# The normalised inputs of a hybrid encoder layer: rebuilt for every projection, or kept in DRAM as two fp16 parts

## The chip, the cores and the metric

One core of a Trainium2 chip. The metric is the device time of one execution in microseconds (us). The engines are TensorE (PE, with its weight loads PEld), VectorE (DVE), ScalarE (ACT), GpSimd (POOL) and SyncE (SP, which here only issues DMAs); 16 DMA engines move data between SBUF and DRAM.

## The reference

One layer of an encoder trunk and a final RMSNorm, on two requests: "p" with 2048 tokens and "s" with 4096, model width 1024, all in fp32.

```python
h = rms_norm(x, norm_g)
proj = h @ w_in                      # columns are split among three groups of heads, A, B and C
shifted = centred_token_shift(proj[..., :TSHIFT_W], tshift_mu)
y_a = rwkv7_branch(...)              # A: two delta-rule scans, forward and backward
y_b = dilated_mixture(rope(b_q), rope(b_k), b_v)
y_c = banded_attention(rope(c_q), rope(c_k), c_v, 128, sink=attn_sink)
mix = concat([y_a * silu(a_g), y_b * silu(b_g), y_c * silu(c_g)])
out = rms_norm(x + mix @ w_out, final_g)
```

## The kernel before

The program runs in four stages. **Stage one** (`stage1`, L309) splits the weights into two fp16 parts, normalises x and makes the ten 128-column projections of group A, in 12 blocks of 512 tokens. `norm_xhat` (L94) loads a block of the transposed x as eight fp32 tiles of 128 channels, sums the squares, makes the row factors `rs`, stores them to DRAM (`sq.RS`, L124) and calls `split_xhat` (L136) for each tile: multiply x by `rs` (L141, on DVE for odd tiles, on POOL for even ones), copy the product to fp16 as the high part (L142, ACT), and subtract that from the product to get the low part (L143, DVE). A projection is then three products of fp16 parts, 24 matmuls (`project`, L166).

**Stage two** (`stage_rwkv`, L870) runs two scan chains of group A (forward and backward) beside `stage_project` (L1127), which makes the projections of group B (`b_project`, L966), fetches the weights of C into the same buffer, and makes those of C (`c_project`, L911). Both go through 24 steps of PB = 256 tokens. `run_all` (L809) emits the three generators in the ratio 7, 7, 1; the instructions are then put in order by the framework's scheduler, which works out an order for each engine, so that matmuls of a projection stand between those of the scans. Each engine and the SP queue work through their own lists in order.

Both projections take their inputs from `load_xhat` (L151). For one step it loads the row factors, broadcast to 128 partitions (L157), and eight fp32 tiles of 128x256 (L161, four buffers), and calls `split_xhat` again: 9 DMAs on SP, 4 multiplications on DVE and 4 on POOL, 8 copies on ACT and 8 subtractions on DVE. B's very first step is prepared near the end of stage one (L383) into a spare part of the weight buffer, so 47 of the 48 calls lie in stage two. The high and low parts have 16 buffers each, which is two steps. **Stage three** (`stage_attend`) does the attention of B and C, **stage four** (`stage_out`) the output projection and the last norm.

Of the kernel before, what the change touches and what calls it, by code (L numbers as in the profile page):

```python
# [7 lines left out]
F32 = mybir.dt.float32  # L8
F32R = mybir.dt.float32r
F16 = mybir.dt.float16  # L10
# [8 lines left out]
NK = 8  # L19
BLK = 512  # L20
# [72 lines left out]

def norm_xhat(env, sq, b, pool, psp, out, quick=False):  # L94


    nc = env.nc
    nm = f"{sq.n}{b}"
    tok = slice(b * BLK, (b + 1) * BLK)
    rs = pool.tile([128, BLK], F32, tag="rs", name=f"rs{nm}", bufs=1)  # L100
    xs = []
    acc = rs
    for k in range(NK):
        xs.append(env.xpool.tile([128, BLK], F32, tag="xt", name=f"xt{nm}{k}", bufs=8))
        env.dma().dma_start(xs[k], sq.xT[128 * k:128 * k + 128, tok]) if quick else \
            nc.sync.dma_start(xs[k], sq.xT[128 * k:128 * k + 128, tok])
        s = acc if k == 0 else pool.tile([128, BLK], F32, tag="tmp", name=f"sq{nm}{k}", bufs=6)
        nc.scalar.activation(s, xs[k], AF.Square)
        if k:
            (nc.vector if quick else nc.gpsimd).tensor_tensor(acc, acc, s, ALU.add)  # L110
    yield
    ps = psp.tile([128, BLK], F32, tag="ps", name=f"pss{nm}")
    for t in range(4):
        for r in (0, 64):
            nc.tensor.matmul(ps[r:r + 64, t:t + 1], acc[:, 128 * t + r:128 * t + r + 64], env.ones[:, 0:1], start=True, stop=True)
    ms = pool.tile([128, 8], F32, tag="ms", name=f"ms{nm}")
    nc.vector.tensor_scalar(ms[:, 0:4], ps[:, 0:4], 2.0 ** -28, 1e-5 * 2.0 ** -18, op0=ALU.mult, op1=ALU.add)
    nc.gpsimd.tensor_tensor(ms[:, 4:8], ms[:, 0:4], env.mhalf[:, 0:4], ALU.pow)
    yield
    ps = psp.tile([128, BLK], F32, tag="ps", name=f"psr{nm}")  # L120
    for t in range(4):
        nc.tensor.transpose(ps[:, 128 * t:128 * t + 128], ms[:, 4 + t:5 + t].to_broadcast([128, 128]), env.ident)
    nc.scalar.activation(rs, ps, AF.Copy)
    nc.sync.dma_start(sq.RS[:, tok], rs[0:1, :])  # L124
    lows = []
    for k in range(NK):
        low = split_xhat(env, pool, xs[k], rs, k, f"{nm}{k}", 16, out, later=quick)
        if quick:
            lows.append(low)
        if k % 2 or quick:  # L130
            yield
    for low in lows:
        low()


def split_xhat(env, pool, xt, rs, k, nm, nx, out, place=None, later=False):  # L136
    nc = env.nc
    n = xt.shape[1]
    xh, xl = place or (pool.tile([128, n], F16, tag=t, name=f"{t}{nm}", bufs=nx) for t in ("xh", "xl"))
    e = nc.vector if k % 2 else nc.gpsimd  # L140
    e.tensor_tensor(xt, xt, rs, ALU.mult)  # L141
    nc.scalar.activation(xh, xt, AF.Copy)  # L142
    low = lambda: nc.vector.tensor_tensor(xl, xt, xh, ALU.subtract)  # L143
    if not later:
        low()
    out[0].append(xh)
    out[1].append(xl)
    return low


def load_xhat(env, sq, b, pool, nx, n, xpool=None, place=None):  # L151

    nc = env.nc
    nm = f"{sq.n}{b}"
    tok = slice(b * n, (b + 1) * n)
    rs = pool.tile([128, n], F32, tag="rs", name=f"rs{nm}f", bufs=1)
    nc.sync.dma_start(rs, sq.RS[0:1, tok].to_broadcast([128, n]))  # L157
    out = [], []
    for k in range(NK):
        xt = (xpool or pool).tile([128, n], F32, tag="xt", name=f"xt{nm}{k}f", bufs=8 if xpool else 4)  # L160
        nc.sync.dma_start(xt, sq.xT[128 * k:128 * k + 128, tok])  # L161
        split_xhat(env, pool, xt, rs, k, f"{nm}{k}f", nx, out, place and [p[k] for p in place])
    return out


def project(env, ps, wh, wl, c0, xh, xl):  # L166
# [142 lines left out]
def stage1(env, seqs):  # L309
    nc, tc = env.nc, env.tc  # L310
    with tc.tile_pool(name="s1st", bufs=2, reuse_waits="tile") as st, \
# [8 lines left out]
        with tc.tile_pool(name="s1", bufs=2, reuse_waits="tile") as pool, tc.tile_pool(name="s1o", bufs=1, reuse_waits="tile") as op:  # L320
# [4 lines left out]
            later = [x for w in (env.WC, env.WB) for x in [split_ahead(env, w, st, psp)]]  # L325
            xhat = [([], []) for _ in blocks]
# [12 lines left out]
            nxt, shifts, raw = None, [], None  # L339

            def step():
                if shifts and next(shifts[0], 0) == 0:
                    shifts.pop(0)

            for n, e in jobs:
                sq, b = blocks[n]
                nb = sq.T // BLK
                nm = f"{sq.n}{b}"
                if e == 0:
                    for _ in nxt or ():  # L350
                        pass
                    nxt = norm_xhat(env, *blocks[n + 1], pool, psp, xhat[n + 1]) if n + 1 < N else None
                    last, raw = raw, pool.tile([128, 8, BLK + 2], F32, tag="raw", name="raw" + nm)
                    if b == 0:
                        nc.gpsimd.memset(raw[:, :, 0:1], 0.0)
                    if b == nb - 1:
                        nc.gpsimd.memset(raw[:, :, BLK + 1:BLK + 2], 0.0)
                if n == 0 and e == 8:
                    weight_scales(env, W)
                if n == 1 and e == 2:  # L360
                    lora_weights(env, W, pool, psp)
                ps = acc.tile([128, BLK], F32, tag="acc", name=f"pj{nm}_{e}")
                project(env, ps, W.h, W.l, 128 * e, *xhat[n])
                if e < 8:
                    nc.scalar.activation(raw[:, e, 1:BLK + 1], ps, AF.Copy, scale=W.f[:, e // 4:e // 4 + 1])
                else:
                    gate = pool.tile([128, BLK], F32, tag="gate", name=f"gate{nm}_{e}", bufs=1)
                    silu_gate(env, pool, gate, ps, W.fh[:, 2:3], f"{nm}_{e}")
                    nc.sync.dma_start(sq.GA[b][:, e - 8], gate)
                if nxt and e > 0:  # L370
                    next(nxt, 0)
                if n == 0 and e < 6:
                    next(own)
                elif n and later and next(later[0], 0) == 0:
                    later.pop(0)
                    if not later:
                        fetch_weights(env, env.WB)
                if e in (1, 3, 5, 8, 9):
                    step()
                if n == N - 1 and e == FIRST:  # L380

                    spare = env.wbuf[:, 16384:20480].rearrange("p (i k t) -> p i k t", i=2, k=NK)
                    env.ready = load_xhat(env, seqs[0], 0, pool, 16, PB, env.xpool, [[spare[:, i, k] for k in range(NK)] for i in range(2)])  # L383
                if e == 7:
                    while shifts:
                        step()
                    if b:
                        nc.gpsimd.tensor_copy(last[:, :, BLK + 1:BLK + 2], raw[:, :, 1:2])
                        nc.gpsimd.tensor_copy(raw[:, :, 0:1], last[:, :, BLK:BLK + 1])
                        shifts.append(shift_a(env, sq, b - 1, last, pool, op, psp))  # L390
                        step()
                    if b == nb - 1:
                        shifts.append(shift_a(env, sq, b, raw, pool, op, psp))
# [514 lines left out]
PB = 256  # L908


def c_project(env, seqs, W, pool, acc):  # L911

    nc = env.nc
    steps = [(sq, b) for sq in seqs for b in range(sq.T // PB)]
    nxt = load_xhat(env, *steps[0], pool, 16, PB)
    for n, (sq, b) in enumerate(steps):
        xh, xl = nxt
        nm = f"c{sq.n}{b}"
        tok = slice(b * PB, (b + 1) * PB)
        t = lambda tag, n_: pool.tile([128, PB], F32, tag=tag, name=n_ + nm, bufs=1)  # L920
# [23 lines left out]
            nc.sync.dma_start(sq.KC[:, half, :, tok], o)  # L944
        yield
        if n + 1 < len(steps):
            nxt = load_xhat(env, *steps[n + 1], pool, 16, PB)
        for g in range(4):
            ps = proj(5 + g)
            gate = pool.tile([128, PB], F32, tag="gate", name=f"g{g}{nm}", bufs=1)  # L950
# [15 lines left out]
def b_project(env, seqs, W, pool, acc):  # L966

    nc = env.nc
    steps = [(sq, b) for sq in seqs for b in range(sq.T // PB)]
    nxt = env.ready  # L970
    for n, (sq, b) in enumerate(steps):
        xh, xl = nxt
        nm = f"b{sq.n}{b}"
        tok = slice(b * PB, (b + 1) * PB)
# [15 lines left out]
            for half, o in enumerate(rope(env, pool, ts[0], ts[1], cs[:, 0], cs[:, 1], f"{i}{nm}")):  # L990
                nc.sync.dma_start(sq.QKB[i, :, half, :, tok], o)
        if n + 1 < len(steps):
            nxt = load_xhat(env, *steps[n + 1], pool, 16, PB)
        for g in range(2):
            ps = proj(4 + g)
            gate = pool.tile([128, PB], F32, tag="gate", name=f"g{g}{nm}", bufs=1)
# [523 lines left out]
def setup(tc, ctx, I, seqs):  # L1520
    env = Env()
    nc = tc.nc
# [4 lines left out]
    dp = env.dp = ctx.enter_context(tc.tile_pool(name="dram", bufs=1, space=DRAM))  # L1527
# [19 lines left out]
    for sq in seqs:  # L1547
        T, nb, n = sq.T, sq.T // BLK, sq.n
        sq.half_done = set()
        sq.RS = dp.tile([1, T], F32, name="RS" + n)  # L1550
        sq.RKX = [dp.tile([128, 6, BLK], F32, name=f"RKX{n}{b}") for b in range(nb)]

        sq.LH = [[dp.tile([128, BLK // RB, 2, RB], F16, name=f"LH{n}{d}{b}") for b in range(nb)] for d in range(2)]
# [125 lines left out]
```

## Time and profile before

| what | us |
|---|---|
| median of 3 runs | 5016.49 |
| lowest and highest of them | 5013.58, 5037.6 |
| the profiled execution, its own time | 5009.68 |
| its span, first to last instruction | 5007.9 |
| PE, DVE, ACT, POOL busy in the span | 4714.6, 3649.6, 2505.7, 2233.0 |

The profile is of one execution. Its page gives busy time by engine, the span in 40 slices, and the costliest groups of instructions by the line of the kernel that issued them; the trace behind it answers questions on one line, one stretch, the waits, or the chain of work that ended last. A matmul is counted as busy from its start to its end, and matmuls overlap in the pipeline. Names of tiles end in p or s for the request; `xts65f` is the x tile 5 of step 6 of request s in `load_xhat`, `xls` and `xhs` are its low and high parts.

### The profile page before, as it was taken

The page shows a single profiled execution, that of the slowest core. Times are in us where ns is not written, and L with a number is a line of the kernel's source. Part 1 is how long each engine was busy: PE and PEld are TensorE (multiplying, and loading weights), DVE is VectorE, ACT ScalarE, POOL GpSimd, SP SyncE. Part 2 cuts the span into 40 slices and gives each one's busy share as a digit, 9 for nine tenths or more (in the row PEclk, how much of TensorE's full clock was granted, in tenths as well). Part 3 has the DMA queues.
Part 4 walks back from the last instruction along what each step waited for, and adds up shares of the span by engine and source line. Part 5 has one row for each costly group of instructions (what it writes and reads, how often), then busy time and mean ns, then how long its engine had stood idle before and what let it go on. Part 6 is the DMA issues. An engine that isn't in the chain of part 4 may idle for free. (4 is left out here: it accounts for less than half of the span.)

```text
span 5007.9 us, 126792 instructions
## 1 busy us (share of the span) xinstructions
PE 4714.6 (94%) x49240; PEld 3667.3 (73%) x49240; DVE 3649.6 (73%) x9212; ACT 2505.7 (50%) x6231; POOL 2233.0 (45%) x3115
## 2 busy tenths in 40 slices
PE   7999999999999999999999899989999999999999
PEld 3444447787777777777777777778888878888887
DVE  6754556778888887788888878858777777765542
ACT  4544544555444555554444444437777667752221
POOL 3555554545555554555556556632232332313210
PEclk9999999999999999999999999999999999999999
DMA  4622233222333233222223232256675665557642
GB/s 140 233 93 97 96 99 112 82 86 86 92 92 93 81 87 112 71 75 71 84 86 89 84 88 87 79 131 140 141 151 123 144 135 117 126 155 239 201 161 91
DMA packets 775924, 569.81 MB, mean 114 GB/s; under 512 B 317836, under 2 KB 693132, under 8 KB 774296
## 3 DMA queue, kind: packets, MB, share of 16 engines
q1 hardware_dynamic: 763608, 528.15, 38.5%
q10 hardware_dynamic: 11712, 33.56, 2.0%
q8 instruction: 386, 6.32, 0.5%
q14 instruction: 218, 1.79, 0.1%
HBM read 380.98 MB, written 180.54 MB: 112 GB/s over the span
## 5 line engine op out<-in xcount | busy, mean ns | idle before, releaser
L172 PEld LDWEIGHTS <-wbuf 128*128 128x128 f16 x8640 | 806.5, 100 | 150.1 <-issue 25.4
L172 PEld LDWEIGHTS <-wh_a 128*128 128x128 f16 x1920 | 188.2, 99 | 227.3 <-issue 8.3
L623 POOL TENSOR_TENSOR ats<-ats,atmask_sb 128x512 f32<-128x512 f32 x128 | 152.4, 1199 | 130.4 <-ACT ats L622 129.5
L1229 ACT ACTIVATE bsms<-bsms,obs 128x256 f32<-128x256 f32 x384 | 179.0, 501 | 31.6 <-DVE obs L1226 31.1
L724 ACT ACTIVATE Ds<-Ss,decs 128x128 f32<-128x128 f32 x256 | 101.3, 397 | 155.1 <-DVE Ss L746 154.5
L172 PEld LDWEIGHTS <-wl_a 128*128 128x128 f16 x960 | 94.1, 98 | 110.5 <-issue 2.7
L1222 PE MATMUL bss<-bkh_sb,bq_sb 128*128 128x256 f32 x384 | 159.9, 423 | 15.0 <-DVE cst0s L1069 9.2
L1226 DVE CUSTOM_DVE_ANT_0 bsms<-bss,bmask_sb 128x256 f32<-128x256 f32 x384 | 148.6, 418 | 25.1 <-PE bpts L1237 11.8
L678 PEld LDWEIGHTS <-Z_sb 128*128 128x128 f16 x1920 | 132.8, 98 | 46.2 <-issue 41.7
L172 PE MATMUL pjs<-xhs,wh_a 128*128 128x512 f16 x640 | 153.6, 381 | 0.0
L1471 DVE TENSOR_TENSOR xs<-xs,os 128x512 f32<-128x512 f32 x64 | 44.0, 687 | 149.9 <-PE os L1465 148.9
L172 PE MATMUL pjs<-xhs,wl_a 128*128 128x512 f16 x640 | 152.5, 379 | 0.0
L1474 ACT ACTIVATE sqs<-xs 128x1024 f32<-128x1024 f32 x32 | 33.8, 1058 | 236.9 <-DVE xs L1471 228.3
L172 PE MATMUL pjs<-xls,wh_a 128*128 128x512 f16 x640 | 151.5, 379 | 0.0
L664 PEld LDWEIGHTS <-NH_sb 128*128 128x128 f16 x1920 | 106.7, 98 | 48.0 <-issue 31.1
L1222 PE MATMUL bss<-bkl_sb,bq_sb 128*128 128x256 f32 x384 | 138.8, 368 | 0.0
L1252 PE MATMUL bpos<-bvs,bpqs 128*64 128x65 f32 x3072 | 135.0, 231 | 1.3 <-DVE bpqs L1241 1.3
L1252 PEld LDWEIGHTS bpos<-bvs,bpqs 128*64 128x64 f32 x3072 | 107.9, 140 | 37.4 <-issue 25.5
L1476 POOL TENSOR_TENSOR osts<-osts,mhalf_sb 128x1 f32<-128x1 f32 x32 | 18.3, 572 | 260.1 <-DVE osts L1475 260.1
L746 DVE SCALAR_TENSOR_TENSOR Ss<-pchs,decs,Ds 64x64 f32<-64x64 f32 x512 | 122.8, 279 | 13.5 <-PE pchs L742 10.4
L1465 PE MATMUL os<-woh,mhs 128*128 128x512 f32 x512 | 126.9, 390 | 0.0
L1465 PE MATMUL os<-woh,mls 128*128 128x512 f32 x512 | 126.5, 389 | 0.0
(3315 smaller groups left out, 17969.9 us busy)
## 6 DMA issues: line engine op xcount, KB each, us to landing
lds<-RKXs SPq DMA_DIRECT2D x64, 384.0 KB
xts<-in_xT_s SPq DMA_DIRECT2D x64, 256.0 KB
bxs<-QKBs SPq DMA_DIRECT2D x64, 256.0 KB
mxs<-MIXs SPq DMA_DIRECT2D x32, 512.0 KB
xs<-in_x_s ACTq DMA_DIRECT2D x32, 512.0 KB
out_s<-xs SPq DMA_DIRECT2D x32, 512.0 KB
ldp<-RKXp SPq DMA_DIRECT2D x32, 384.0 KB
OBs<-obs SPq DMA_DIRECT2D x32, 264.0 KB
```

What stands on the lines that cost most here:

```text
L172: nc.tensor.matmul(ps, w[:, k, c0:c0 + 128], x[k], start=(n == 0), stop=(n == 23))
L623: nc.gpsimd.tensor_tensor(at[:, h], at[:, h], mask, ALU.mult)
L664: nc.tensor.matmul(z4[:, u, :], NH[:, u, :], half_runs(TU[:, 0, u, :], oT, w), start=True, stop=True)
L678: nc.tensor.matmul(pt[:, 1, u, :], Z[:, u, :], half_runs(TU[:, 1, u, :], oU, w), start=True, stop=True)
L724: nc.scalar.activation(S2[:, hp], S[:, hp], AF.Copy, scale=G.dec[:, hp, c:c + 1])
L746: nc.vector.scalar_tensor_tensor(S[half[h], hp, d], pp[half[h], hp], G.dec[half[h], hp, c:c + 1], S2[half[h], hp, d], op0=ALU.mult, op1=AL ...
L1222: nc.tensor.matmul(ps[:, u, :nk], q[:, qa:qa + 128 * d - d + 1:d], kt[:, ka:ka + nk * d - d + 1:d], start=(n == 0), stop=(n == 1))
L1226: nc.vector.tensor_tensor_reduce(sm[:, u, :nk], ps[:, u, :nk], env.bmask[:, (128 * i - win[i]) // 64, :nk], 1.0, 1e30, ALU.add, ALU.min, o ...
L1229: nc.scalar.activation(sm[:, u, :nk], sm[:, u, :nk], AF.Exp, scale=-1.0, bias=ob[:, o + u, 65:66])
L1252: nc.tensor.matmul(pos[0][r:r + 64, 2 * (a % 2) + u], pq[:, u, j + r:j + r + 64], V[:, ns * ph + place[win[i] + j]], start=(j == 0), stop= ...
L1465: nc.tensor.matmul(pss[t, hf], a[:, k, 128 * t:128 * t + 128], w[:, k, 512 * hf:512 * hf + 512], start=(i == 0 and k == OUT_K[0]), stop=(i ...
L1471: nc.vector.tensor_tensor(x[:, cols], x[:, cols], pss[t, hf], ALU.add)
```

## The change

Stage one stores both fp16 parts of each block to DRAM (`keep_xhat`), and `load_xhat` becomes one DMA of 1 MB per step from there into a tile with two buffers. The row factors are no longer stored. `stage1` calls `keep_xhat` after each of a block's first eight projections, which makes 16 DMAs of 128 KB a block, in runs of 512 bytes. In DRAM a step's data lie as 8 KB in a row for each partition.

```diff
@@ norm_xhat
-    nc.sync.dma_start(sq.RS[:, tok], rs[0:1, :])
...
-def load_xhat(env, sq, b, pool, nx, n, xpool=None, place=None):
...
-    nc.sync.dma_start(rs, sq.RS[0:1, tok].to_broadcast([128, n]))
-    out = [], []
-    for k in range(NK):
-        xt = (xpool or pool).tile([128, n], F32, tag="xt", name=f"xt{nm}{k}f", bufs=8 if xpool else 4)
-        nc.sync.dma_start(xt, sq.xT[128 * k:128 * k + 128, tok])
-        split_xhat(env, pool, xt, rs, k, f"{nm}{k}f", nx, out, place and [p[k] for p in place])
-    return out
+def keep_xhat(env, sq, b, xhat, k):
+    for i in range(2):
+        env.nc.sync.dma_start(sq.XH[b][:, :, i, k, :], xhat[i][k].rearrange("p (h t) -> p h t", t=PB))
+def load_xhat(env, sq, b, pool, place=None):
+    x = place if place is not None else pool.tile([128, 2, NK, PB], F16, tag="x", name=f"x{sq.n}{b}f", bufs=2)
+    h = BLK // PB
+    env.nc.sync.dma_start(x, sq.XH[b // h][:, b % h])
+    return [[x[:, i, k] for k in range(NK)] for i in range(2)]
...
@@ stage1, after projection e of block n
+                if e < NK:
+                    keep_xhat(env, sq, b, xhat[n], e)
...
@@ setup
-        sq.RS = dp.tile([1, T], F32, name="RS" + n)
+        sq.XH = [dp.tile([128, BLK // PB, 2, NK, PB], F16, name=f"XH{n}{b}") for b in range(nb)]
```

## Rows read from the trace of the kernel before

**Rows 1.** Busy time by stretch: us, busy (count) of each engine, clock, DMA share, GB/s

```profile
core 0: us, PE busy (x) PEld busy (x) DVE busy (x) ACT busy (x) POOL busy (x), PEclk, DMA share, GB/s
0.00:735.00 735.00, 686.09 (x3688) 330.33 (x3688) 430.41 (x666) 353.59 (x582) 364.68 (x274) 0.99 0.37 125
735.00:3325.00 2590.00, 2429.19 (x29805) 1960.81 (x29806) 2121.91 (x5411) 1262.26 (x3709) 1424.51 (x2208) 0.97 0.30 87
3325.00:4460.00 1135.00, 1064.25 (x13311) 933.51 (x13309) 829.91 (x2764) 774.64 (x1762) 327.89 (x418) 0.97 0.61 134
```

**Rows 2.** Three short stretches, same columns

```profile
125.00:250.00 125.00, 115.49 (x613) 55.14 (x612) 97.90 (x177) 70.16 (x119) 63.50 (x47) 0.95 0.69 233
...
500.00:600.00 100.00, 100.00 (x564) 49.08 (x563) 54.79 (x67) 49.55 (x81) 57.00 (x43) 1.00 0.29 96
...
4300.00:4400.00 100.00, 99.61 (x1310) 88.24 (x1309) 72.84 (x258) 73.53 (x168) 23.93 (x40) 1.00 0.45 99
```

**Rows 3.** The chain that ended last, 2720 to 3320 us, by line

```profile
by line: PE jcs L172 15.5%; issue 5.2%; PE cvcs L182 4.0%; DVE TUs L682 2.8%; DVE Z_sb L666 2.3%; DVE Ss L746 2.2%; PE pA0s L618 2.1%; PE pA1s L618 1.7%; PE pchs L721 1.6%; PE pchs L729 1.5%; DVE tas L567 1.4%; PE pchs L734 1.3%; DMA KCs<-r
```

**Rows 4.** Pieces of that chain: start us, us, what

```profile
2747.20 0.32 DVE xls60f L143
2749.10 2.53 DMA xts65f<-in_xT_s
...
3283.27 2.56 DMA xts155f<-in_xT_s
...
3289.27 0.41 DVE xls157f L143
```

**Rows 5.** Lines 141, 142, 143 in stage two: us, busy (count) of DVE and POOL; ACT; DVE

```profile
735.00:3325.00 2590.00, 116.45 (x188) 150.84 (x188) 0.97 0.30 87
...
735.00:3325.00 2590.00, 138.59 (x376) 0.97 0.30 87
...
735.00:3325.00 2590.00, 188.80 (x376) 0.97 0.30 87
```

**Rows 6.** Single instructions of lines 141 and 143: ns min/median/max, start us

```profile
L141 POOL TENSOR_TENSOR xtp06f<-xtp06f,rsp0f x1: 903/903/903, 659.7 to 659.7; 128x256 f32<-128x256 f32 x1
...
L143 DVE TENSOR_TENSOR wbuf<-xtp01f,wbuf x1: 945/945/945, 659.9 to 659.9; 128x256 f16<-128x256 f32 x1
...
L143 DVE TENSOR_TENSOR wbuf<-xtp02f,wbuf x1: 413/413/413, 661.5 to 661.5; 128x256 f16<-128x256 f32 x1
```

**Rows 7.** DMA issues on SP by line: ns min/median/max, first and last start us

```profile
L157 SPq DMA_DIRECT2D rss0f<-RSs x2: 326/326/327, 1028.2 to 2329.1; - x2
...
L161 SPq DMA_DIRECT2D xts01f<-in_xT_s x2: 382/382/382, 1029.5 to 2329.5; - x2
...
L306 SPq DMA_DIRECT2D wbuf<-wdr00w_b x1: 582/582/582, 200.1 to 200.1; - x1
...
L294 SPq DMA_DIRECT2D wdr00w_c<-wbuf x1: 319/319/319, 125.4 to 125.4; - x1
```

**Rows 8.** PE's longest waits in stage one: us in total, times, longest us

```profile
PE pssp L115 <- DVE rsp L110: 18.1, 1, 18.1
PE wpt L62 <- DVE wm L59: 6.3, 1, 6.3
```

**Rows 9.** Stores that end a step of B and of C: ns, first and last start us

```profile
L1006 SPq DMA_DIRECT2D VBs<-vbs x16: 377/385/1029, 1165.8 to 1906.0; - x16
...
L960 SPq DMA_DIRECT2D VCs<-vcs x16: 370/384/592, 2501.3 to 3361.4; - x16
```

**Rows 10.** Longest waits at SP's head in stage two: us in total, times, longest us

```profile
SPq L524 <- PE pws L541: 87.2, 34, 7.3
SPq L524 <- PE pwp L541: 53.7, 14, 8.0
```

**Rows 11.** A transfer of 512 KB in the chain, stage four: start us, us, what

```profile
4483.73 10.64 DMA mxp<-MIXp
```

More of the change, by code (lines that the diff above doesn't have):

```diff
@@ L133, in norm_xhat, with split_xhat @@
         low()
-def split_xhat(env, pool, xt, rs, k, nm, nx, out, place=None, later=False):
+def split_xhat(env, pool, xt, rs, k, nm, nx, out, later=False):
     nc = env.nc
     n = xt.shape[1]
-    xh, xl = place or (pool.tile([128, n], F16, tag=t, name=f"{t}{nm}", bufs=nx) for t in ("xh", "xl"))
+    xh, xl = (pool.tile([128, n], F16, tag=t, name=f"{t}{nm}", bufs=nx) for t in ("xh", "xl"))
     e = nc.vector if k % 2 else nc.gpsimd
@@ L148, in split_xhat @@
     return low
-def load_xhat(env, sq, b, pool, nx, n, xpool=None, place=None):
[L153 to L156, printed above, removed]
-    nc.sync.dma_start(rs, sq.RS[0:1, tok].to_broadcast([128, n]))
-    out = [], []
-    for k in range(NK):
-        xt = (xpool or pool).tile([128, n], F32, tag="xt", name=f"xt{nm}{k}f", bufs=8 if xpool else 4)
-        nc.sync.dma_start(xt, sq.xT[128 * k:128 * k + 128, tok])
-        split_xhat(env, pool, xt, rs, k, f"{nm}{k}f", nx, out, place and [p[k] for p in place])
-    return out
+def keep_xhat(env, sq, b, xhat, k):
[6 more added lines that the diff above has]
+    return [[x[:, i, k] for k in range(NK)] for i in range(2)]
 def project(env, ps, wh, wl, c0, xh, xl):
@@ L379, in stage1 @@
                     step()
+                if e < NK:
+                    keep_xhat(env, sq, b, xhat[n], e)
                 if n == N - 1 and e == FIRST:
                     spare = env.wbuf[:, 16384:20480].rearrange("p (i k t) -> p i k t", i=2, k=NK)
-                    env.ready = load_xhat(env, seqs[0], 0, pool, 16, PB, env.xpool, [[spare[:, i, k] for k in range(NK)] for i in range(2)])
+                    env.ready = load_xhat(env, seqs[0], 0, pool, spare)
                 if e == 7:
@@ L914, in c_project @@
     steps = [(sq, b) for sq in seqs for b in range(sq.T // PB)]
-    nxt = load_xhat(env, *steps[0], pool, 16, PB)
+    nxt = load_xhat(env, *steps[0], pool)
     for n, (sq, b) in enumerate(steps):
@@ L946, in c_project @@
         if n + 1 < len(steps):
-            nxt = load_xhat(env, *steps[n + 1], pool, 16, PB)
+            nxt = load_xhat(env, *steps[n + 1], pool)
         for g in range(4):
@@ L992, in b_project @@
         if n + 1 < len(steps):
-            nxt = load_xhat(env, *steps[n + 1], pool, 16, PB)
+            nxt = load_xhat(env, *steps[n + 1], pool)
         for g in range(2):
```

## The prediction

> **What bounds the kernel now.** I read the busy time by stage first, then the chain of work that ended last, then the lines that the change touches. The work to be removed lies in stage two, 735 to 3325 us, over half of the span. There PE is busy for 94% (2429.2 of 2590), but its weight loads only for 76% (1960.8), and DVE for 82% (2121.9) [rows 1]. In the attention stage the order is another: weight loads 82%, DVE 73% [rows 1], and in its best 100 us the weight loads reach 88% [rows 2]. So in stage two PE and DVE hold each other up: neither is full, and where DVE is less loaded PE gets further. The chain says the same. It was followed back to about 2720 us, and in its last 600 us of stage two the projections' matmuls have 15.5% + 4.0%, while single lines of the scans have 1 to 3% each [rows 3]. The lines of load_xhat are on it too: 14 loads of x tiles, the first 2.53 us and the last 2.56 us, 38.6 us in sum; 54 pieces of the subtraction on DVE (0.32 us the first, 0.41 us the last), 20.8 us; the multiplication with 13.2 us; some 2 us in smaller pieces [rows 4]. In all 74.7 us of 600, or 12%.
>
> **Removed from stage two.** 47 calls of load_xhat. Their DVE work is 116.5 us of multiplications and 188.8 us of subtractions, together 305 of DVE's 2122 us; POOL loses 150.8 of 1425 us and ACT 138.6 of 1262 us [rows 1, 5]. SP loses 47 x (0.33 + 8 x 0.38) = 158 us of issuing and gets 47 x 0.58 = 27 us for the 1 MB loads [rows 7]. ACT (49% busy) and POOL (55%) were not full [rows 1], so I count their savings at nothing in themselves.
>
> POOL's saving acts on DVE, though. At 659.9 us, beside a POOL multiplication that ran from 659.7 for 0.90 us, a subtraction on DVE took 945 ns; the same one at 661.5 us, after it, took 413 ns [rows 6]. DVE thus lost (945 - 413)/945 = 56% of its speed beside POOL. 150.8 us less POOL work is worth at most 0.56 x 150.8 = 85 us of DVE, if DVE did that kind of work all the time, and at least nothing. I take half, 43 us, since DVE is not always busy and many of its operations read PSUM. The Trainium skill's GPSIMD Engine Reference, section Specifications, has this as a rule: GpSimd shares its SBUF interfaces with VectorE, and contends with DVE instructions that run in a 2-port mode or read two SBUF inputs. If it held for every DVE instruction of the stage, the sum would take the 85 us, and if POOL did not matter, the 0; the two durations speak for the rule.
>
> **What that is worth.** Upper bounds: the chain's 12% of 2590 us is 322 us; all of DVE's saving, 305 + 85 = 390 us; the weight loads at the best density seen, 1960.8/0.88 = 2222 us for the stage, 368 us less. Lower bound: nothing, where the scans' own sequence sets the pace (a rival below). For the value I draw a line through the two stages that show PE and DVE at work together: from 82% DVE and 75.7% weight loads to 73% and 82.2% [rows 1], that is 0.74 points of weight loads gained for each point of DVE given up. In a stage of T us the weight loads have 1960.8/T and DVE (2121.9 - 305 - 43)/T = 1774/T. Setting 1960.8/T = 0.757 + 0.74 x (0.819 - 1774/T) gives T = 2400 us: **190 us less**, with weight loads at 82% and DVE at 74%. This is the attention stage's state, and about six tenths of the chain's share, which is reasonable, as other pieces move into its place. What is late next is the rest of DVE's work for the scans (L682, L666, L746), which PE waits for.
>
> **Added in stage two.** One 1 MB load per step. Its landing is not in the trace; bounds are 1 MB at the highest rate of stage one, 233 GB/s [rows 2], 4.5 us, and twice the 10.6 us that a 512 KB transfer took [rows 11], 21 us. A step lasts (1906.0 - 1165.8)/15 = 49 us in B and 57 us in C [rows 9], and with two buffers the load can go out as soon as the step before the running one has ended, so even 21 us are hidden. I count nothing. If that cover is gone (the load goes out late in the step) up to 21 us a step come back; that is the slower rival's place.
>
> **Added in stage one.** 192 stores, 25.2 MB, at about 0.32 us of SP each [rows 7], 61 us of issuing in 735 us, less the twelve small stores of row factors. Stage one moves 125 GB/s on average [rows 1] and 233 at its peak [rows 2]; 25.2 MB in 700 us add 36. The stores read tiles that were made a block earlier, so they don't wait, and the next writer of those buffers comes a block later. Behind them on SP stand the x loads of a next block and the scans' inputs. PE is 100% busy from 500 to 600 us [rows 2], and its two longest waits in the stage, 18.1 and 6.3 us, come at the start [rows 8], before there is anything to store. The worst would be that each of 12 blocks starts late by its 16 issues, 12 x 5.1 = 61 us; the best is nothing, as PE is full where one split falls away. I take 5 us, near the low end, by the full slice.
>
> **The sum.** 5009.7 - 190 + 5 = 4825 us for the profiled execution. The median of the runs is 6.8 us above that execution, so the prediction is 4832 us. The clock is left out: it was granted at 0.97 in stage two and in the attention stage, and at 1.00 where PE was full [rows 1, 2].
>
> **The rivals.**
> - **PE is full already.** Read by its matmuls, PE is idle for only 161 us in stage two [rows 1]. If only that can go, and about half of it does, the gain is 80 us less the 5: 4941 us. For it: 94% busy. Against it: matmuls overlap, and the weight loads stand at 76%. The Trainium skill, page Perfetto Trace Analysis, section Identifying the Most-Contended Engine, says that matmul busy time is no good measure and to judge by the weight loads; by it this rival falls and the forecast stands. Chance 0.2.
> - **The whole share of the chain goes.** 322 us less, plus 5: 4700 us. For it: waits for x tiles also hold up what stands behind them on DVE and ACT. Against: it needs DVE at 1774/2268 = 78% beside weight loads at 86%, which no stage shows. Chance 0.13.
> - **The scans' sequence sets the pace** and projections only fill gaps, so removing their work gives nothing: 5021 us. For it: 7 steps of each scan are emitted for one of a projection. Against: on the chain the projections' matmuls are the largest entry, and the scan's state update (L746) has 2.2% [rows 3]. Chance 0.08.
> - **Slower: the 1 MB load blocks SP.** It must wait for the last matmul of an earlier step, and SP's list is in order: a load placed too early holds the scans' inputs and all stores behind it. The waits at SP's head for the load of a scan's input are up to 8.0 us now, 2.9 us on average (141 in 48) [rows 10]. If every step stalled the scans for the 8.0 us, 47 x 8 = 376 us would go against the 190: 5016 + 376 - 185 = 5207 us. It decides from 185/47 = 3.9 us a step. Against: x loads wait on SP today as well, eight a step. Chance 0.07.
>
> **How the numbers follow.** The forecast has the remaining 0.52. A measurement of this kernel can tell about 0.5%, 25 us, from no change. Faster by more than that: forecast, full PE, whole share, 0.85; within: the scans' pace, 0.08; slower: 0.07. The range goes from 4690 us, just under the whole share, to 4950 us, just above the full PE; what is left out is the scans' pace and the blocked SP, and little beyond the low end.
>
> **What would show it.** Right: no L141 to L143 in stage two; DVE near 1770 to 1815 us of a stage of some 2400 us; weight loads at 80% or more; attention and output stages as long as now; stage one within 10 us of 735. Wrong: weight loads still at 76% with DVE at 70% (the scans' pace), a new SP wait for the x tile of several us a step, or PE idle in stage one behind x loads.

## The result and the profile after

The changed kernel takes **4842.38 us** (median of 4 runs, 4832.77 to 4849.22), against 5017.33 us before (4 runs): ratio 0.9642, 95% interval 0.9611 to 0.9673. That is 175 us less and inside the forecast's range. The profiled execution took 4842.48 us, with a span of 4840.7 us, which is 167 us under the span of before.

First the busy time by stretch, with the columns of [rows 1]. The stretches are stage one, stage two (up to the last matmul of C, which ends at 3188.9 us), its last 100 us, the attention stage and the output stage.

```profile
0.00:735.00 735.00, 685.70 (x3688) 330.31 (x3688) 425.77 (x651) 349.60 (x572) 361.77 (x268) 0.99 0.48 158
735.00:3190.00 2455.00, 2384.49 (x30002) 1954.57 (x30002) 1851.09 (x4868) 1157.77 (x3352) 1276.23 (x2033) 0.99 0.32 93
3090.00:3190.00 100.00, 82.18 (x794) 72.07 (x793) 34.21 (x68) 24.12 (x51) 30.06 (x29) 0.95 0.55 146
3190.00:4296.00 1106.00, 1043.92 (x13178) 916.91 (x13178) 813.64 (x2750) 766.34 (x1750) 311.51 (x407) 0.98 0.60 131
4296.00:4840.00 544.00, 532.41 (x2372) 440.75 (x2372) 266.36 (x370) 112.73 (x175) 116.93 (x216) 0.99 0.58 182
```

The second row of [rows 1] stops at 3325 us, while C's last matmul of before ends at 3360.6. Over the same work as above, the kernel before reads:

```profile
735.00:3361.00 2626.00, 2452.17 (x30000) 1980.25 (x30000) 2133.31 (x5428) 1271.81 (x3726) 1441.23 (x2219) 0.97 0.31 89
```

All of the gain lies in stage two: 2626 us became 2455. Stage one ends at 733.8 us (731.1 before), and the attention stage lasts 1106 us (1102), both by PE's last matmuls. Two things shrank together. PE's idle time fell from 174 to 71 us, 103 less. Summed over all lines of the views of PE's waits, those that a DVE instruction ended fell from 116 us to 31, which is 85 of the 103, and all others from 56 to 38. One of these waits of the scans, before and after (us in total, times, longest us):

```profile
PE pchs L729 <- DVE Us L708: 14.0, 12, 2.7
...
PE pchs L728 <- DVE Us L707: 6.5, 6, 1.6
```

And the same 30,000 matmuls were busy for 2384 us where they had been busy for 2452, 68 less, while the clock was granted at 0.99 and not 0.97. DVE went from 81.2% to 75.4% of the stage, the weight loads from 75.4% to 79.6%.

The chain that ended last, 2550 to 3150 us, by line, answers to [rows 3]:

```profile
by line: PE jcs L169 21.3%; issue 7.2%; PE cvcs L179 3.3%; DVE Ss L745 2.1%; DMA GCs<-g0cs 2.0%; DMA QCs<-rp2q1cs 2.0%; PE pA1s L617 1.8%; PE pchs L728 1.8%; PE pA0s L617 1.7%; PE pchs L720 1.7%; DVE TUs L681 1.7%; PE pchs L733 1.5%; DMA QC
```

The projections' matmuls (jcs, cvcs) went from 19.5% to 24.6%. Of load_xhat nothing stands there, no subtraction and no landing of an x tile, where [rows 4] had them. In their place came stores of the rotated queries and gates (QCs, GCs).

Next the issues on SP of the new lines (ns min/median/max, first and last start us): two of the 1 MB loads at L159, then two rows of the stores at L152.

```profile
L159 SPq DMA_DIRECT2D xp4f<-XHp x2: 320/322/325, 859.9 to 2034.2; - x2
...
L159 SPq DMA_DIRECT2D xp7f<-XHp x2: 319/320/320, 1008.5 to 2224.7; - x2
...
L152 SPq DMA_DIRECT2D XHs<-xhs x64: 512/572/1373, 264.3 to 661.9; - x64
...
L152 SPq DMA_DIRECT2D XHp<-xlp x32: 513/596/659, 35.1 to 222.3; - x32
```

SP's waits in stage two (us in total, times, longest) for its most frequent cause, and the longest waits of the new load, those with cvb in B and those with cvc in C:

```profile
SPq L523 <- PE pws L540: 146.0, 45, 8.5
SPq L523 <- PE pwp L540: 86.9, 21, 8.7
...
SPq L159 <- PE cvbs L179: 28.3, 10, 6.6
SPq L159 <- PE cvcp L179: 21.1, 5, 9.8
SPq L159 <- PE cvbp L179: 9.8, 5, 3.8
SPq L159 <- PE cvcs L179: 8.9, 5, 3.7
```

So the wait that the slower rival feared is there. Those four lines are 68 us in 25 waits; with seven shorter ones it is 77 us on SP, 1.6 us a step over 47 steps.

### The profile page after: what moved, and what is told of

It reads as the page before. It is cut to its first block, busy times and chain, and to the rows that moved or that the text cites. A ratio compares the mean times of both kernels' runs of the same rounds, so it can differ in the third digit from the quotient of the medians.

```text
span 4840.7 us, 124914 instructions
## 1 busy us (share of the span) xinstructions
PE 4646.5 (96%) x49240; PEld 3642.5 (75%) x49240; DVE 3356.8 (69%) x8636; ACT 2386.4 (49%) x5847; POOL 2066.4 (43%) x2923
## 4 chain that ended last, share of the span: by engine, by line
PE 73%; DVE 10%; DMA 7%; issue 3%; POOL 3%; ACT 2%; SPq 1%; DVEq 0%; POOLq 0%; ACTq 0%
PE pjs L169 8%; PE os L1464 7%; PE jbs L169 4%; PE jcs L169 4%; PE jcp L169 3%; PE op L1464 3%; PE bss L1221 3%; PE jbp L169 2%; PE bpos L1251 2%; PE pjp L169 2%; PE bpts L1236 2%; PE cvbs L179 2%; PE bsp L1221 1%; DMA bxs<-QKBs 1%; PE pA0s L617 1%
## 5 line engine op out<-in xcount | busy, mean ns | idle before, releaser
L1464 PE MATMUL os<-wol,mhs 128*128 128x512 f32 x512 | 126.5, 389 | 0.0
```

Of the source, the lines that this page charges most:

```text
L1464: nc.tensor.matmul(pss[t, hf], a[:, k, 128 * t:128 * t + 128], w[:, k, 512 * hf:512 * hf + 512], start=(i == 0 and k == OUT_K[0]), stop=(i ...
```

## The experiments

Three kinds of kernel were run: the kernel before with one part of the change (e1), the changed kernel with a part of the old work put back, and the changed kernel emitted in another ratio (e8, e12). Nothing reads what the put-back lines make, so those kernels do more than the reference asks and leave nothing out. All ratios are to the kernel before on the same chip. A difference between two kernels is that of their ratios times 5017 us; with half-intervals of about 0.003 and 0.0025 it is uncertain by some 20 us.

In the summary, stage two is the length from the end of stage one to C's last matmul, weight loads and DVE are busy times in it, and the last column is explained in the section on why. These four columns are of one profiled execution each, which for most lies within 12 us of the median; that of e1 lies 21 us under it and that of e6 16 us over it.

| kernel | median us | ratio | against after | stage two | weight loads | DVE | line gives |
|---|---|---|---|---|---|---|---|
| before | 5017.33 | 1 | +180 | 2626 | 1980 | 2133 | 2611 |
| after | 4842.38 | 0.9642 | 0 | 2455 | 1955 | 1851 | 2439 |
| e1 stores only | 5050.47 | 1.0044 | +202 | 2625 | 1978 | 2131 | 2608 |
| e2 DVE work back | 4975.93 | 0.9899 | +129 | 2579 | 1972 | 2098 | 2586 |
| e10 half of e2 | 4916.42 | 0.9806 | +82 | 2518 | 1959 | 2008 | 2527 |
| e3 POOL work back | 4866.06 | 0.9689 | +24 | 2474 | 1953 | 1894 | 2461 |
| e4 ACT work back | 4885.17 | 0.9727 | +43 | 2495 | 1963 | 1870 | 2456 |
| e11 twice e4 | 4833.59 | 0.9641 | 0 | 2446 | 1946 | 1856 | 2435 |
| e6 all three back | 5000.63 | 0.9951 | +155 | 2608 | 1987 | 2139 | 2619 |
| e5 loads, unpaced | 4953.53 | 0.9865 | +112 | 2563 | 1963 | 1867 | 2454 |
| e9 loads, paced | 4912.43 | 0.9798 | +78 | 2537 | 1966 | 1860 | 2452 |
| e7 old load_xhat beside | 5093.18 | 1.0138 | +249 | 2677 | 2005 | 2137 | 2631 |
| e8 ratio 6, 6, 1 | 4881.01 | 0.9712 | +35 | 2497 | 1963 | 1877 | 2459 |
| e12 ratio 8, 8, 1 | 4850.36 | 0.9671 | +15 | 2460 | 1956 | 1859 | 2445 |

**e1: the stores alone.** The kernel before with keep_xhat and its DRAM tiles:

```diff
+                if e < NK:
+                    keep_xhat(env, sq, b, xhat[n], e)
...
+        sq.XH = [dp.tile([128, BLK // PB, 2, NK, PB], F16, name=f"XH{n}{b}") for b in range(nb)]
```

> The kernel before with the 192 stores of the fp16 parts added in stage one; nobody reads them, and stage two prepares its inputs as before. Theory (the stores hide under a full PE): 5 us more than before, 5022 us, stage one within 10 us of its 731 us. Rival (the stores delay the x loads of the next block on SP): up to 61 us more, 5078 us, with PE idle in stage one.

Measured: ratio 1.0044 (1.0022 to 1.0067), 22 us more, with 11 us either way. Stage one ended at 744.9 us:

```profile
0.00:745.00 745.00, 692.56 (x3688) 333.71 (x3688) 429.49 (x661) 351.77 (x579) 365.20 (x272) 0.98 0.48 155
745.00:3370.00 2625.00, 2444.97 (x30000) 1977.53 (x30000) 2131.35 (x5433) 1272.76 (x3727) 1446.31 (x2221) 0.97 0.31 89
```

Stage two is as before (2625 us). The stores themselves cost from 3 us (in the changed kernel) to 14 us (here) of stage one; e2, e3 and e4, on the same chip and with the same stores, ended it at 737 to 740 us. The profiled execution is the fastest of e1's seven, so where the rest of the 22 us lies its profile doesn't show.

**e2: DVE's work back, and e10: half of it.** In load_xhat, behind the 1 MB load, with xc a constant tile:

```diff
+    if place is None:
+        again(env, sq, b, pool, x)
...
+    for k in range(NK):
+        e = nc.vector if k % 2 else nc.gpsimd
+        if k % 2:
...
+            e.tensor_tensor(xm, xc, xc, ALU.mult)
...
+        nc.vector.tensor_tensor(xl, xc, x[:, 0, k], ALU.subtract)
```

e10 has the multiplication where k % 4 is 1 and the subtraction where k is even.

> The kernel after, with DVE's share of the old preparation put back on constants: in each of the 47 steps of stage two 4 multiplications and 8 subtractions of 128x256 on DVE, whose results nobody reads; no loads, no ACT, no POOL work. Theory (the gain is DVE's time): 305 of the 348 us of DVE that the forecast counted come back, so some 305/348 of the 175 us gained, 153 us: about 4995 us. Rival (the gain is the waits for x tiles and for the other engines, and the work itself fits into DVE's idle time): at most 50 us come back, under 4892 us.

> The kernel after with half of DVE's old share put back on constants: 2 multiplications and 4 subtractions in each of the 47 steps. Theory (each us of DVE costs about the same, 124/305 = 0.4): 62 us more than the kernel after, ratio to before 0.977. Rival (a threshold: DVE costs only once it is the fullest engine, above some 80% of the stage): 30 us or less, ratio 0.970.

Measured: +129 us for the whole and +82 us for half. Stage two of e2:

```profile
737.00:3316.00 2579.00, 2431.53 (x30002) 1972.39 (x30001) 2098.27 (x5434) 1155.94 (x3351) 1311.99 (x2033) 0.97 0.30 89
```

And of e10:

```profile
739.00:3257.00 2518.00, 2402.30 (x29994) 1958.85 (x29995) 2008.23 (x5152) 1156.38 (x3351) 1296.87 (x2032) 0.98 0.31 91
```

DVE gained 247 and 157 us of busy time, and each us of it came with 0.52 us of time both times (129/247, 82/157). The equality is in part chance, for each difference is uncertain by some 20 us. Reckoned by the work put back, 302 us in e2 and 153 in e10, it is 0.43 and 0.54; in e10 the other DVE instructions were busy 33 us longer too, and no line that was put back explains it. The rival of e10, a threshold near 80% of the stage, did not show: with DVE at 80% (2008 of 2518) the 82 us were already there. DVE's work counts although DVE is never full. In e2 the waits of PE that DVE ended are back, at 101 us (31 in the changed kernel, 116 before).

One limit of all put-back kernels belongs here. The multiplications have constant inputs, so nothing holds them to their step: all 188 ran in the first 300 us of e2's stage two. The subtractions, which read the loaded tile, were spread over it. Busy time of DVE, first the multiplications' line, then the subtractions':

```profile
737.00:1037.00 300.00, 97.28 (x188) 0.95 0.33 100
1037.00:3316.00 2279.00, 0.00 (x0) 0.98 0.30 87
...
737.00:1037.00 300.00, 26.44 (x56) 0.95 0.33 100
1037.00:3316.00 2279.00, 181.65 (x320) 0.98 0.30 87
```

**e3: POOL's work back.** The same loop with the multiplications of even k on POOL alone.

```diff
+    for k in range(NK):
+        e = nc.vector if k % 2 else nc.gpsimd
+        if k % 2 == 0:
...
+            e.tensor_tensor(xm, xc, xc, ALU.mult)
```

> The kernel after, with only POOL's share put back on constants: 4 multiplications of 128x256 in each of the 47 steps, results unread. Theory (POOL costs through DVE, which runs slower beside it): 43 of 348 us of DVE, some 22 us of the gain, 4864 us, and longer DVE instructions in the trace. Rival (POOL's own time mattered not at all, nor its effect on DVE): 4842 us.

Measured: +24 us. The work ran in the first 600 us of stage two, where DVE shows what it does. The first 300 us of the changed kernel:

```profile
735.00:1035.00 300.00, 289.74 (x3459) 236.05 (x3459) 207.08 (x557) 149.94 (x432) 148.09 (x238) 0.98 0.35 105
```

And of e3, then its stage two:

```profile
735.00:1035.00 300.00, 279.92 (x3265) 226.28 (x3264) 226.03 (x532) 145.12 (x410) 231.00 (x375) 0.98 0.35 106
...
738.00:3212.00 2474.00, 2391.76 (x29985) 1953.05 (x29984) 1894.31 (x4872) 1159.23 (x3352) 1396.14 (x2221) 0.99 0.31 93
```

With POOL busy for 231 us of 300, and not 148, DVE took 226 us for fewer instructions than the 207 us had held: 425 ns each, not 372. Over the stage DVE was busy 43 us longer with the same instructions (1894.3 against 1851.1). Its +24 us is only just outside the uncertainty, but the place fits. In the first 600 us of stage two, where all of the work ran, the changed kernel and e3 read:

```profile
734.00:1334.00 600.00, 587.60 (x7250) 481.40 (x7251) 435.39 (x1170) 294.53 (x847) 303.65 (x498) 0.99 0.33 99
...
740.00:1340.00 600.00, 576.22 (x7035) 468.33 (x7036) 459.55 (x1130) 287.45 (x828) 410.81 (x669) 0.99 0.32 96
```

e3 made 215 matmuls fewer there, about 18 us at the rate of the first row. DVE took 407 ns per instruction there, against 372, and 383 ns in both kernels behind it.

**e4: ACT's work back, and e11: twice that.** The conversion to fp16 in the loop, once or twice per tile:

```diff
+    for k in range(NK):
...
+        nc.scalar.activation(xh, xc, AF.Copy)
```

> The kernel after, with only ACT's share put back on constants: 8 copies to fp16 of 128x256 in each of the 47 steps, results unread. Theory (ACT has room, 49% busy): 4842 us, within 15 us. Rival (work on any engine that feeds the scans delays them, full or not): 139 us of ACT come back as a good part of the gain, 4900 us or more.

> The kernel after with twice ACT's old share put back on constants: 16 copies in each of the 47 steps, 278 us or more of ACT. The eight copies cost 43 us by the ratio, at an ACT that was half idle. Theory (time on ACT costs in proportion, as its instructions stand in order with the scans'): some 86 us, ratio to before 0.981. Rival (the 43 us were a less lucky order of the instructions): 20 to 50 us, ratio 0.968 to 0.974.

Measured: +43 us for the work once, 0 (4833.59 us, ratio 0.9641) for it twice. Stage two of e4:

```profile
740.00:3235.00 2495.00, 2407.86 (x29995) 1963.37 (x29996) 1869.84 (x4870) 1283.64 (x3727) 1279.06 (x2032) 0.98 0.31 92
```

And of e11:

```profile
737.00:3183.00 2446.00, 2376.93 (x30002) 1946.04 (x30002) 1856.02 (x4870) 1411.81 (x4104) 1277.42 (x2033) 0.99 0.32 94
```

e4 missed the 15 us of its theory, and e11 both of its cases. ACT had 254 us more to do in e11 than in the changed kernel, and the stage was 9 us shorter. So the 43 us of e4 are not a price that grows with ACT's work. The first 600 us of stage two in e4, then in e11, say the same:

```profile
740.00:1340.00 600.00, 583.48 (x7074) 473.34 (x7075) 429.96 (x1136) 414.81 (x1205) 294.97 (x482) 0.99 0.32 96
...
737.00:1337.00 600.00, 583.73 (x7151) 476.53 (x7152) 433.26 (x1147) 513.08 (x1499) 297.79 (x486) 0.99 0.33 99
```

All of e4's conversions ran there, and it was 176 matmuls behind the changed kernel's 7250, about 15 us; e11, with nearly twice the work done by then, was 99 behind, about 8 us. The other 25 us of e4's stage came later, where none of the added instructions ran, and e11 made its 8 us good. What else differs is the order: the added lines shift it, and the list of PE's instructions in e4 and in e11 is that of the changed kernel through stage one and departs from it at the first projection of stage two. I take from it that one variant can lie some 40 us off by its order; how this order costs 25 us and more was not shown.

**e6: all three back at once**, without the old loads.

```diff
+    for k in range(NK):
+        e = nc.vector if k % 2 else nc.gpsimd
...
+        e.tensor_tensor(xm, xc, xc, ALU.mult)
...
+        nc.scalar.activation(xh, xc, AF.Copy)
...
+        nc.vector.tensor_tensor(xl, xc, x[:, 0, k], ALU.subtract)
```

> The kernel after, with the work of DVE, ACT and POOL put back together on constants, no loads and no waits between them. Theory (the costs add): 124 + 41 + 19 = 184 us more in stage two, ratio to before about 1.000. Rival (they overlap, the largest decides): 124 to 140 us more, ratio 0.99.

Measured: +155 us. Stage two:

```profile
740.00:3348.00 2608.00, 2452.07 (x29990) 1986.70 (x29991) 2138.81 (x5428) 1280.65 (x3723) 1426.37 (x2212) 0.96 0.29 85
```

DVE, ACT and POOL have the busy times of before again, and PE's waits that DVE ended are 105 us. With ACT at the 0 of e11 the parts add up, 129 for DVE and 24 for POOL, 153 in all; with the 43 of e4 they would make 196. Each part is uncertain by some 20 us, so this sum agrees with the costs adding, but doesn't prove it.

**e5: the old loads back, and e9: the same, paced.** Nine loads a step, one broadcast row (of x, in place of the factors) and eight tiles of x, beside the 1 MB load; e9 adds five one-column operations on POOL that need the loaded tiles and those of the step. The edit of e5:

```diff
+    nc.sync.dma_start(rs, env.I["xT_" + sq.n][0:1, tok].to_broadcast([128, PB]))
+    for k in range(NK):
...
+        nc.sync.dma_start(xt, sq.xT[128 * k:128 * k + 128, tok])
```

> The kernel after, with only the nine loads of the old preparation put back: in each of the 47 steps one broadcast row and eight fp32 tiles of 128x256 into four buffers, 423 DMAs and 158 us of SP's issuing, read by nobody. Theory (DVE, ACT and POOL work explain the whole gain: 124 + 41 + 19 of the 174 us that stage two lost, by the runs before): within 15 us of the kernel after, ratio to before 0.961 to 0.968. Rival (SP's issuing and the landing of x tiles held up the scans; they were 38.6 of the 74.7 us on the chain): 174 x 38.6/74.7 = 90 us more, ratio 0.98.

> The kernel after with the nine loads of the old preparation put back, as before, but held to the pace of the steps: five one-column POOL operations per step read the loaded tiles together with the step's own input, so a buffer comes free only when its step has been loaded. In the earlier run with loads alone nothing held them back; they were all issued between 800 and 1200 us, at a DMA share of 0.65, and all of its loss lay there. Theory (at the steps' pace loads cost little): at most 30 us more than the kernel after, ratio to before 0.970 or less. Rival (158 us of SP's issuing and the queueing of loads cost in themselves): 90 us or more, ratio 0.982 or more.

Measured: +112 us for e5, +78 us for e9. In e5 nothing held the loads to their step, and the profile shows them crowded. Two stretches of it:

```profile
900.00:1000.00 100.00, 81.85 (x1013) 66.85 (x1010) 52.93 (x142) 37.68 (x107) 36.59 (x59) 0.93 0.65 194
...
1400.00:1500.00 100.00, 96.51 (x1196) 78.15 (x1197) 83.50 (x215) 45.34 (x130) 58.53 (x95) 1.00 0.32 97
```

The loads were issued from 750 to 1218 us. In that time, with the DMA engines at 0.65, every other engine does less; with the usual 0.32 it is over. SP's list stood for 101 us at the tile loads (L163), and from 800 to 1200 us one line of DVE waited 52 us until stores of the gates had landed (`g1bp` <- `GBp`). So the 112 us, though above the 90 of the rival, are the price of a crowd and not of the old loads. e9 spread them over the stage:

```profile
737.00:3274.00 2537.00, 2416.95 (x29996) 1966.09 (x29995) 1860.10 (x4869) 1159.08 (x3352) 1316.87 (x2268) 0.98 0.38 112
```

DVE has nearly the busy time of the changed kernel, and still the stage is 82 us longer. That lies between the theory (at most 30) and the rival (90 or more). It is no clean price of the loads either: the pacing operations stand in POOL's list and hold it up until their tiles are there. On those two lines POOL waited 175 us for DMAs in 90 waits, 84 us of them for tiles of x and 78 for the 1 MB load of a step. The longest group:

```profile
POOL xms140f L166 <- DMA xs14f<-XHs: 27.2, 2, 23.7
```

How the 78 us divide into the loads and this pacing, e9 can't tell.

**e7: the whole old load_xhat beside the new load.** The row of factors is the first row of x here.

```diff
+    nc.sync.dma_start(rs, env.I["xT_" + sq.n][0:1, tok].to_broadcast([128, PB]))
+    for k in range(NK):
...
+        nc.sync.dma_start(xt, sq.xT[128 * k:128 * k + 128, tok])
...
+        e.tensor_tensor(xt, xt, rs, ALU.mult)
+        nc.scalar.activation(xh, xt, AF.Copy)
+        nc.vector.tensor_tensor(xl, xt, xh, ALU.subtract)
```

> The kernel after, with the whole old preparation beside it, loads and waits among the three engines included, results unread (the row factor is replaced by a row of x). Theory (work, not waits): as the run with the work of the three engines put back, ratio to before 1.000 plus or minus 0.006. Rival (waits count as well): 1.01 or more.

Measured: +249 us, 69 us slower than before, ratio 1.0138, which the rival named. Work and paced loads alone, e6 and e9, make 155 + 78 = 233. But here too the placement is not that of before. ACT's conversions, first to 1835 us, then after it, and the whole stage in the same two parts:

```profile
742.00:1835.00 1093.00, 156.19 (x376) 0.93 0.44 132
1835.00:3419.00 1584.00, 0.00 (x0) 0.98 0.28 84
...
742.00:1835.00 1093.00, 951.71 (x10469) 748.66 (x10467) 910.59 (x2220) 539.48 (x1551) 616.35 (x899) 0.93 0.44 132
1835.00:3419.00 1584.00, 1534.51 (x19528) 1256.28 (x19526) 1226.71 (x3207) 747.04 (x2173) 824.89 (x1315) 0.98 0.28 84
```

All of the old work ran in the first 1100 us, where PE stood at 87%. So the 47 us by which e7 exceeds e1 (1.0138 against 1.0044) are not the price of the 47 loads of 1 MB: crowding is in them.

**e8 and e12: another mix of scans and projections.** In the changed kernel RATIO = (7, 7, 1) says how many scan steps are emitted for one of a projection. In its last 100 us C runs almost alone (the third row of the profile after), so two more experiments looked for a better version.

```diff
-RATIO = (7, 7, 1)
+RATIO = (6, 6, 1)
```

e12 has (8, 8, 1).

> The kernel after, emitted in the ratio 6, 6, 1 instead of 7, 7, 1. In the kernel after the scans end at 3091 us and C's projections at 3189 us; before, 3315 and 3361 us. Theory (the lighter projections left the two sides out of balance, and the last 98 us have too little beside them): 20 to 50 us less than the kernel after, ratio to before 0.955 to 0.960. Rival (the tail is full enough, PE does the same matmuls anyway): within 10 us of the kernel after, ratio 0.962 to 0.966.

> The kernel after, emitted in the ratio 8, 8, 1 instead of 7, 7, 1. With 6, 6, 1 the scans ended at 3143 instead of 3091 us and C's projections at 3238 instead of 3189 us: fewer steps of the scans per step of a projection made both later. Theory (the scans should go first, projections fill in): 10 to 40 us less than the kernel after, ratio to before 0.956 to 0.962. Rival (7, 7, 1 is the better mix; either side costs): 10 us or more above the kernel after, ratio 0.966 or more.

Measured: +35 us and +15 us; the gains expected of e8 and of e12 did not come. For e8, stage two and the part of it behind the last scan:

```profile
740.00:3238.00 2498.00, 2404.08 (x30008) 1963.18 (x30006) 1877.96 (x4870) 1166.07 (x3354) 1281.23 (x2034) 0.98 0.31 92
3143.00:3238.00 95.00, 83.61 (x787) 73.17 (x784) 33.68 (x66) 24.24 (x51) 30.22 (x29) 0.95 0.55 152
```

The tail is as long as with 7, 7, 1 (95 and 98 us), and the scans end later (3143 and 3091 us). With 8, 8, 1 the tail is 65 us, but the scans end at 3136. The +15 us of e12 are within the uncertainty. No version that was run beats the changed kernel; e11 equals it.

## Why the prediction was right

The time came out 10 us over the forecast of 4832, in the case that had most of the chance. By its steps:

- **DVE and PE hold each other up, and the line through two stages gives the rate.** Held. The forecast drew 0.74 points of weight loads per point of DVE; the stage went 4.2 points up for 5.8 down, which is 0.72. The last column of the table is that line, T = (weight loads + 0.74 x DVE) / 1.363 (1.363 is 0.757 + 0.74 x 0.819), with each kernel's own busy times. Before and after lie 15 and 16 us above it, and the line gives 172 us between them where 171 were measured. Every kernel without extra transfers lies within 17 us of it, except e4 and e8 (38 or 39 us above; I put it down to their order, which was not shown). Those with extra transfers lie above it by 46 (e7), 85 (e9) and 109 us (e5): this is time that does not go through DVE. That DVE's work held PE up is shown more directly by PE's waits that DVE ended: 116 us before, 31 after, and 101 again with DVE's work put back (e2). The line takes the weight loads' measured time, so it explains a result more easily than it foretells one.
- **DVE loses 305 us, and 43 more by POOL's relief.** Both terms were too large. DVE's busy time fell by 282 us (2133.3 to 1851.1) and not by 348. The instructions of L141 to L143 are gone, 302 us of busy time by their own records, but the records of neighbours on DVE overlap. Three of them in the kernel before (start us, us, what):

```profile
1064.98 0.42 DVE L143 TENSOR_TENSOR xls00f<-xts00f,xhs00f 128x256 f16<-128x256 f32 x1 [0.99 <-PE cvbp L182]
1065.33 0.42 DVE L143 TENSOR_TENSOR xls01f<-xts01f,xhs01f 128x256 f16<-128x256 f32 x1
1065.66 0.68 DVE L682 TENSOR_TENSOR TUp<-TUp,pt2p 128x512 f16<-128x512 f16 x1
```

  A subtraction is on record for 0.42 us, but the next instruction starts 0.33 to 0.35 us after it. Over stage two the removed records overlap the others by 42 us, so their going freed 259 us. The relief was 23 us: without the removed lines, DVE's records cover 1874 us before and 1851 after. That is about half of the 43, and such sums differ by as much between kernels with the same work on POOL (1884 in e10). 259 + 23 = 282. With 282 in place of 348 the line gives (1980.25 + 0.74 x 1851.1) / 1.363 = 2458 us, 153 less than its 2611 for before, and e6 found 155 for this work on its own. So the 190 were 35 to 37 too many. That POOL's work slows DVE is real: e3 put the multiplications back and DVE was busy 43 us longer, nearly all of it where they ran. The rule cited from the Trainium skill, GPSIMD Engine Reference, section Specifications, that the two contend, agrees with e3's 425 against 372 ns.
- **The clock left out.** Here lies what made up for half of it, and that is luck. The same 30,000 weight loads were busy 1980 us at a clock of 0.97 and 1955 us at 0.99; in the line these 26 us are worth 19. This was not in the sum, and with it 153 becomes 172. Without this second error, of the other sign, the stage would have been some 153 us shorter, not 171, against the 190 of the forecast; the total would still have been within the range.
- **ACT's saving counted at nothing, POOL's only by way of DVE.** Held for ACT, as far as the scatter of orders lets one see: e11 did 254 us more of it in the same time, e4 did 126 us more and came out at +43. For POOL the sum had 0.74 x 43 / 1.363 = 23 us. e3 measured 24, but for work that was packed into 600 us; the relief of 23 us found above is worth 12 by the line.
- **Old loads counted at nothing, new ones at nothing.** Only their difference is shown to be small: the gain of 180 us (by the ratio), plus the stores' 3 to 22, less the work's 155, leaves 28 to 47 us for the exchange of nine loads for one and the waits that went with them, at an uncertainty of some 20 and with orders that scatter by 40. The line puts the exchange at nothing (15 and 16 us above it). Of SP's issuing, the new loads took 0.33 us each at the median and not the 0.58 of the sum. e9's 78 us are for loads on top of the new ones, with their pacing. That the chain named landings for 38.6 of its 74.7 us on load_xhat was thus no price. What one load of 1 MB costs stays open.
- **Stores in stage one, +5.** The trace of the changed kernel has +3, e1 +14, its ratio +22 with 11 either way; within the bounds of 0 to 61. The issue was mis-sized: 0.51 us at least and 0.57 to 0.6 at the median, not 0.32, so the 192 took 120 us of SP in all and not 61, and PE hardly noticed.
- **The rivals.** PE full already: it had half of PE's idle time going, 80 us of the 161 in [rows 1], and nothing else. Over the whole of stage two 103 of 174 idle us went, and the stage became 171 us shorter. As the rule of the Trainium skill (Perfetto Trace Analysis, Identifying the Most-Contended Engine) had it, matmul busy time was no measure of what was left: busy time itself went down by the other 68 us. The whole share of the chain (322 us): 171 came. The scans' pace: it had nothing going. The blocked SP: its waits are there, 1.6 us a step, under the 3.9 from which they decide.

The signs named ahead mostly came: attention and output as long as before, stage one within 10 us, weight loads at 79.6% (80% or more was named). DVE at 1851 us was outside the 1770 to 1815 named, and that was the sign of the two terms that were too large.

## What to carry to other kernels

When two engines each stand at 75 to 95% in a stage, neither is "the" bound: read how both stand in another stage of the same kernel, draw the line, and expect about half of the work taken off the second engine back (here 0.43 and 0.54 us per us of DVE work put back, whole and half, uncertain by 0.07 and 0.13). Count that work by what it frees: 302 us of records that overlapped their neighbours freed 259. Judge PE's room by its weight loads, and remember that its busy time can shrink with the stalls. Where every edit shifts the order of the instructions, a single variant's difference under some 40 us, 0.8% here, is not a price until a second dose moves it the same way, or the trace shows the loss where the added work ran.

## What the runs showed of the hardware beyond that

The granted clock was the higher, by and large, the busier PE was in a stretch, and so paid a part of the gain. In the first 300 us of stage two, columns as above, the kernel before:

```profile
735.00:1035.00 300.00, 277.12 (x3107) 220.05 (x3108) 219.88 (x569) 149.78 (x432) 155.46 (x236) 0.93 0.34 101
```

And e7:

```profile
735.00:1035.00 300.00, 255.72 (x2567) 196.51 (x2566) 231.70 (x555) 150.36 (x419) 162.60 (x227) 0.90 0.48 142
```

With PE busy for 256, 277 and 290 us of 300 the clock was granted at 0.90, 0.93 and 0.98 (e7, before, after). It is no strict rule: e3 had 0.98 with PE busy for 280. Between the two levels, 1.2 and 2.4 GHz, 0.93 means that PE spent 14% of this stretch at the lower one, and 0.98 that it spent 4%. If the clock follows the stalls, as these rows suggest, a stall that goes pays twice, once as the wait and once as the clock behind it; the two were not tested apart.

On SP, an issue of a 1 MB load took 0.32 us at the least, no more than the small loads of [rows 7], while a store of keep_xhat, with 128 KB (two pieces of 512 bytes in each of 128 partitions), took 0.51 us at the least. A load of eight times the data, in one piece of 8 KB for each partition, was the cheaper issue.

POOL slowed some of DVE's instructions and left others alone. In the changed kernel (ns min/median/max, first and last start us), one product of two SBUF tiles and one that reads a PSUM tile:

```profile
L568 DVE TENSOR_TENSOR bks<-qs,e3s x128: 270/318/1239, 1487.3 to 2993.6; 128x128 f32<-128x128 f32 x128
...
L665 DVE TENSOR_TENSOR Z_sb<-pz1s,lvmask_sb x64: 398/424/427, 1547.8 to 3040.1; 128x256 f16<-128x256 f32 x64
```

By the trace's records in stage two, the first took 280 ns on average in the 26 cases with no POOL record beside it, and 465 ns in the 51 that lay almost wholly beside POOL's. The instructions on `Z_sb` at L665 took 417 and 418 ns.
